# Attention stages of an encoder layer: TensorE order written by hand, softmax sums applied to the outputs

## The chip, the cores and the metric

The kernel runs on one core of one Trainium2 chip, in one launch. The metric is the device time of a run in microseconds (us). The kernel before has a median of 2528.19 us over three runs (2527.29 to 2535.42). Its profiled execution took 2528.55 us, of which the program's instructions span 2526.8 us; all rows below are of that execution.

## The reference

One post-norm encoder layer is applied to two sequences with the same weights: a prompt of 512 tokens and a sample of 1024, both 1024 wide. Per sequence:

```
u     = layernorm(x) * (1 + sc1) + sh1                  # modulation from silu(c) @ w_ada
proj  = u @ w_in  -> qa ka va (8 heads on 2 kv heads of 64) | qb kb vb (8 heads) | ga gb
oa    = softmax(rope(rms(qa)) . rope(rms(ka)) / 8) @ va          # over all tokens ("gqa")
ob    = softmax(qb . kb / 8 + bias) @ vb                          # over an 8 x 16 window ("na")
mixed = (sigmoid(ga) * (oa @ w_out_a) + sigmoid(gb) * (ob @ w_out_b)) @ w_out
x     = layernorm(alpha * x + (1 + g1) * mixed) * g + b
x     = layernorm(alpha * x + (1 + g2) * (relu(mod(x) @ w_ff1) ** 2 @ w_ff2)) * g + b
```

The softmax is `p / sum(p)`; whether the division comes before or after the product with v changes no value but rounding.

## The kernel before, in words

Work is in chunks of 512 tokens: one of the prompt, two of the sample. To keep fp32 precision each matrix product is three products of a high and a low half (`mm3`, L110): `hi*hi`, `hi*lo`, `lo*hi`, 512 columns each, accumulated in one PSUM bank. A weight unit is 128x1024 fp32; `wunit` (L81) loads it on SP's queue, ScalarE rounds it to `whi` (L93), VectorE subtracts for `wlo` (L94). `stream` (L97) keeps one unit ahead.

Every stage is a Python generator that yields its progress, and `weave` (L46) always advances the one that is furthest behind. That fixes the order in which instructions are recorded. The order on each engine is then set at build time by a scheduler that keeps a list of ready instructions by priority, so TensorE's order need not be the recorded one. At run time every engine works through its own list in order and waits on semaphores.

The stages, in order of time:

- Up to 171 us: modulation, and `proj` (L412) of the prompt.
- Stage 1, 171 to 285 us (L1008): `sample_u`, the layer norm and 64 transposes (L167) of the sample; `gates` (L492) of the prompt; `mod_rest`, 22 more modulation columns on VectorE.
- Stage 2, 285 to 640 us (L1023): attention of the prompt, woven with `proj` of the two sample chunks. `gqa` (L503) runs to 470 us, `na` (L598) from 490 us.
- Stage 3, 640 to 1163 us (L1040): attention of the sample, woven with its `gates` and with `out_merge` (L726) of the prompt. `gqa` runs to 942 us, `na` from 968 us.
- After 1163 us: merge, mix and norm of the rest, and the feed-forward layer.

In `gqa` a block is one head and 512 queries. For each of its four query tiles, `softmax` (L528) makes the scores `S` (L535: 2 products of 512 columns per 512 keys), the row maximum `m` on VectorE (L538), the exponential on ScalarE with its row sum `z` (L541), the reciprocal (L542), and multiplies the probabilities `P` by it, in turn on VectorE (L544) and ScalarE (L546). `values` (L549), for each 128 keys of the block before, turns four 128x128 tiles of `P` on TensorE (L553, tile `T`), splits the result into `ph` and `pl` (L556, L557), and multiplies with `V` into `A` (L566, L567).

In `na` an item is one head, 8 rows and 16 columns of the token grid (32 items in the prompt, 64 in the sample). GpSimd adds table and mask to the bias `wm` (L647), three items ahead. `softmax` (L651) makes 2 score products of 256 (prompt) or 384 columns (L658), the sum with the bias and its maximum on VectorE (L661, L662), the exponential (L665), the reciprocal (L666) and the scaling of `P` (L667, VectorE). `values` (L670) turns 2 or 3 tiles (L674), ScalarE copies them to `pt` (L676), and `weigh` (L679) multiplies with `V` (L681, fp32, two records per product in the trace). After four items VectorE copies the result to `o` (L686).

Fill work, that is `proj` and `gates`, has four PSUM banks in stage 2 and three in stage 3 (L1015, L1027). All writes of `g`, `oa` and `ob` are issued by SP.

Of the kernel before, what the change touches and what calls it, by code (L numbers as in the profile page):

```python
# [1 line left out]

# [8 lines left out]
F32 = mybir.dt.float32  # L11
# [21 lines left out]
GL = 0.06  # L33
AHEAD = 1
GQ = (0.55, 0.55)
AT = (1.1, 0.94)
# [3 lines left out]
class Kern:  # L40
# [4 lines left out]
    @staticmethod  # L45
    def weave(*gens):  # L46

        live = [[0.0, i, g] for i, g in enumerate(gens)]
        while live:
            e = min(live)  # L50
            try:
                e[0] = next(e[2]) or 0.0
            except StopIteration:
                live.remove(e)

# [59 lines left out]

    def dps(self):
        return self.psD.tile([P, CH], F32, tag="D", name="D")
# [44 lines left out]
    def mod_tile(self, pool, xns, s, sh0, sc0, kt, vector=False):  # L162

        nc = self.nc
        ps = self.dps()
        for t in range(TT):
            nc.tensor.transpose(ps[:, t * P:(t + 1) * P], xns[t][:, kt * P:(kt + 1) * P], self.ident)  # L167
        u = pool.tile([P, CH], F32, tag="uf", name="uf", bufs=3)
# [5 lines left out]
        return u  # L174
# [118 lines left out]
    def u_tile(self, seq, xns, pool, upool, U, kt):  # L293
        nc = self.nc
        u = self.mod_tile(pool, xns, seq, 0, 8, kt, seq == 0)
# [4 lines left out]
        U.append((uh, ul))  # L300


    def tokmajor(self, U, ws, kper, n, ps):
# [3 lines left out]
        for j in range(nu):  # L307
# [3 lines left out]
            for t in range(TT):  # L311
                for i in range(kper):
                    k = j * kper + i
                    uh, ul = U[k]
                    self.mm3(ps[t][:, :n], (uh[:, t * P:(t + 1) * P], ul[:, t * P:(t + 1) * P]),
                             (hv[:, i, :], lv[:, i, :]), k == 0, k == KT - 1)
            yield
# [9 lines left out]
    def stack(self, pool, src, dsts, scale=None, perm=False):  # L327

        nc = self.nc
        for j in range(2):  # L330
            t = pool.tile([P, CH], F32R, tag="stk", name="stk", bufs=3)
# [74 lines left out]
    def pair_stack(self, pool, q2s, hp, dsts):  # L406
        ps = self.dps()
        for t in range(TT):
            self.nc.tensor.transpose(ps[:, t * P:(t + 1) * P], q2s[t][:, hp * P:(hp + 1) * P], self.ident)
        self.stack(pool, ps, dsts)  # L410

    def proj(self, ch, U, pool):  # L412
# [4 lines left out]
        ws = self.stream([a["wq"][i] for i in range(4)] + [a["wkv"][i] for i in range(2)]  # L417
                         + [a["wst"][i] for i in range(8)] + [a["wvb"][i] for i in range(4)])
# [3 lines left out]
        for _ in self.tokmajor(U, ws, 2, 512, ps):  # L422
            done += 1
            yield done / 18.0
# [9 lines left out]
        for _ in self.tokmajor(U, ws, 4, 256, ps):  # L434
            done += 1
            yield done / 18.0
# [25 lines left out]
        todo = {2: [(q_rope, 0)], 3: [(q_rope, 1), (k_rope, 0)], 4: [(q_rope, 2), (k_rope, 1)],  # L462
                5: [(q_rope, 3), (k_rope, 2)], 6: [(k_rope, 3)],
                7: [(q_stack, 0)], 8: [(q_stack, 1)], 9: [(q_stack, 2)], 10: [(q_stack, 3)], 11: [(k_stack, 0)]}
        for i in range(8):
            ps = self.wstat(next(ws), [U])[0]
# [4 lines left out]
            if i == 2:  # L471
# [5 lines left out]
        ps = []  # L477
        for j, _ in enumerate(self.tokmajor(U, ws, 2, 512, ps)):
            for f, x in todo.get(8 + j, ()):
                f(x)  # L480
            done += 1
            yield done / 18.0
        for t in range(TT):
            v = pool.tile([P, CH], F32, tag="vb", name="vb", bufs=2)
            nc.scalar.activation(v, ps[t], AF.Copy)
            r = t0 // GW + 2 * t
            for hp in range(4):
                for i in range(2):
                    c0 = (r % 4 + i) * GW
                    nc.sync.dma_start(s["vb"][hp][c0:c0 + GW, r // 4], v[i * GW:(i + 1) * GW, hp * P:(hp + 1) * P])  # L490

    def gates(self, chs, Us, pool, func):  # L492
        nc, a = self.nc, self.a
        for i, w in enumerate(self.stream(a["wst"][8 + i] for i in range(16))):
            ps = self.wstat(w, Us)
            for (seq, t0), p in zip(chs, ps):
                g = pool.tile([P, CH], F32, tag="gst", name="gst", bufs=2)
                nc.scalar.activation(g, p, func)
                nc.sync.dma_start(self.scr[seq]["g"][i][:, t0:t0 + CH], g)
# [3 lines left out]
    def gqa(self, seq, pool, psp):  # L503
# [6 lines left out]

        def load(kv, h):
            if kv is not None and kv not in KV:
                K = []
                for r in range(2):
                    k = pool.tile([P, T], F32R, tag=f"K{r}", name="K", bufs=1)
# [10 lines left out]
            return KV[kv][0] if kv is not None else None, Qs[h]  # L526

        def softmax(blk, qt):  # L528
            kv, h, qc = blk
            K, Q = load(kv, h)  # L530
            S = psp.tile([P, T], F32, tag="S", name="S", bufs=2 if nh == 1 else 1)
            q = Q[:, qc * CH + qt * P:qc * CH + (qt + 1) * P]
            for k in range(nh):
                for r in range(2):
                    nc.tensor.matmul(S[:, k * CH:(k + 1) * CH], q, K[r][:, k * CH:(k + 1) * CH],  # L535
                                     start=r == 0, stop=r == 1)
            m = pool.tile([P, 1], F32, tag="m", name="m", bufs=4)
            nc.vector.tensor_reduce(m, S[:, :T], axis=AX.X, op=ALU.max, negate=True)  # L538
            p = pool.tile([P, T], F32, tag="P", name="P", bufs=8 if nh > 1 else 7)
            z = pool.tile([P, 1], F32, tag="z", name="z", bufs=4)  # L540
            nc.scalar.activation(p, S[:, :T], AF.Exp, bias=m, scale=1.0, accum_out=z)  # L541
            nc.vector.reciprocal(z, z)  # L542
            if qt % 2:
# [645 lines left out]
```

## Time and profile before

| | |
|---|---|
| profiled execution / its span | 2528.55 us / 2526.8 us |
| TensorE busy (mean granted clock) | 2388.2 us, 95% (0.975) |
| VectorE / ScalarE / GpSimd busy | 1472.3 / 971.3 / 330.1 us (58 / 38 / 13%) |
| stages 1, 2, 3 | 114, 355, 523 us |

Busy time of TensorE is the union of its matmul records. Records of successive matmuls overlap, so a busy TensorE can still run below its best rate, and the cost of one product is read from the distance between starts, not from its record's length. The granted clock is a share of full speed: 1.00 is the level of 2.4 GHz, and a half is that of 1.2 GHz.

### The profile page before, as it was taken

How to read it: one execution, taken by the hardware profiler on the slowest of the kernel's cores; microseconds unless marked ns; L12 is line 12 of the kernel's file. 1: busy time of each engine (PE TensorE's matmuls, PEld its weight loads, DVE VectorE, ACT ScalarE, POOL GpSimd, SP SyncE). 2: the span in 40 equal slices, each digit the busy share in tenths (PEclk: the TensorE clock that was granted, in tenths of full speed). 3: DMA queues.
4: the chain of work that ended last, by engine and by line, in shares of the span. 5: the costliest groups of instructions: out<-in, count | busy, mean ns of one | idle time of the engine just before them, and what ended most of it. 6: DMA issues, size and time to landing. Idle time of an engine off the chain costs nothing.

```text
span 2526.8 us, 29800 instructions
## 1 busy us (share of the span) xinstructions
PE 2388.2 (95%) x10992; PEld 1898.6 (75%) x10992; DVE 1472.3 (58%) x2511; ACT 971.3 (38%) x1589; POOL 330.1 (13%) x278
## 2 busy tenths in 40 slices
PE   5987899979999999989998999999999999999997
PEld 4876777756777777767776788887788888888876
DVE  7987677565477763575867754445733333333466
ACT  4434456434577763554334223222412211221222
POOL 4210021230000003331202000003100000000133
PEclk9998899989999999999999999999999999999999
DMA  6757744565512117585656525334511210211231
GB/s 248 245 185 238 213 119 145 141 187 174 157 55 66 58 50 184 148 235 189 202 188 206 191 69 159 99 90 126 176 40 45 61 48 26 67 50 34 68 116 59
DMA packets 134851, 325.86 MB, mean 129 GB/s; under 512 B 21392, under 2 KB 34224, under 8 KB 134704
## 3 DMA queue, kind: packets, MB, share of 16 engines
q1 hardware_dynamic: 134128, 322.86, 41.8%
q0 software_dynamic: 288, 1.05, 0.3%
q8 instruction: 87, 1.43, 0.2%
q14 instruction: 60, 0.49, 0.1%
q10 hardware_dynamic: 288, 0.03, 0.0%
HBM read 261.99 MB, written 62.93 MB: 129 GB/s over the span
## 4 chain that ended last, share of the span: by engine, by line
PE 68%; DVE 12%; DMA 8%; issue 4%; ACT 3%; POOL 2%; SPq 1%; POOLq 0%; ACTq 0%; DVEq 0%
PE D L112 18%; PE D L114 18%; PE D L113 18%; PE S L535 3%; PE T L553 3%; DVE wlo L94 2%; PE A L681 2%; PE A L566 2%; PE A L567 1%; DMA wraw<-in_wada 1%; PE T L674 1%; DVE junk L248 1%; DMA wraw<-in_wst 1%; ACT whi L93 1%; PE S L658 1%
## 5 line engine op out<-in xcount | busy, mean ns | idle before, releaser
L93 ACT ACTIVATE whi<-wraw 128x1024 fp32r<-128x1024 f32 x266 | 279.4, 1057 | 828.2 <-PE D L114 396.9
L114 PE MATMUL D<-uh,wlo 128*128 128x512 f32 x1344 | 537.2, 400 | 20.5 <-DVE wlo L94 20.5
L112 PE MATMUL D<-uh,whi 128*128 128x512 f32 x1344 | 538.3, 400 | 14.1 <-ACT whi L93 12.5
L113 PE MATMUL D<-ul,whi 128*128 128x512 f32 x1344 | 533.9, 397 | 0.0
L94 DVE TENSOR_TENSOR wlo<-wraw,whi 128x1024 fp32r<-128x1024 f32 x266 | 334.8, 1261 | 336.5 <-ACT whi L93 325.8
L114 PEld LDWEIGHTS D<-uh,wlo 128*128 128x128 f32 x1344 | 256.5, 191 | 78.9 <-DVE wlo L94 23.0
L112 PE MATMUL D<-whi,hh 128*128 128x512 f32 x768 | 304.8, 398 | 6.3 <-ACT hh L864 6.3
L112 PEld LDWEIGHTS D<-uh,whi 128*128 128x128 f32 x1344 | 257.3, 191 | 70.1 <-ACT whi L93 13.8
L114 PE MATMUL D<-whi,hl 128*128 128x512 f32 x768 | 303.7, 397 | 0.8 <-DVE hl L865 0.6
L113 PE MATMUL D<-wlo,hh 128*128 128x512 f32 x768 | 303.4, 397 | 0.0
L113 PEld LDWEIGHTS D<-ul,whi 128*128 128x128 f32 x1344 | 257.0, 191 | 54.7 <-issue 0.5
L886 DVE TENSOR_TENSOR y<-y,D 128x512 f32<-128x512 f32 x168 | 115.1, 685 | 214.8 <-PE D L114 214.2
L112 PEld LDWEIGHTS D<-whi,hh 128*128 128x128 f32 x768 | 145.4, 189 | 43.8 <-ACT hh L864 10.2
L114 PEld LDWEIGHTS D<-whi,hl 128*128 128x128 f32 x768 | 145.3, 190 | 37.3 <-DVE hl L865 3.7
L113 PEld LDWEIGHTS D<-wlo,hh 128*128 128x128 f32 x768 | 145.5, 189 | 33.6
L847 POOL TENSOR_TENSOR y<-y,g 128x1024 f32<-128x1024 f32 x12 | 28.8, 2402 | 867.4 <-DVE y L886 867.4
L538 DVE TENSOR_REDUCE m<-S 128x1 f32<-128x1024 f32 (+1 forms) x96 | 99.7, 1041 | 51.7 <-PE S L535 51.2
L557 DVE TENSOR_TENSOR pl<-T,ph 128x512 fp32r<-128x512 f32 x160 | 107.4, 684 | 16.4 <-ACT ph L556 15.0
L556 ACT ACTIVATE ph<-T 128x512 fp32r<-128x512 f32 x160 | 93.4, 597 | 55.5 <-PE T L553 53.1
L112 PE MATMUL D<-whi,uh 128*128 128x512 f32 (+1 forms) x288 | 105.5, 371 | 2.8 <-ACT whi L93 2.2
L647 POOL TENSOR_TENSOR wm<-Wb,mask 128x384 f32<-128x384 f32 (+1 forms) x96 | 78.4, 830 | 198.4 <-DVE m L661 118.8
L113 PE MATMUL D<-wlo,uh 128*128 128x512 f32 (+1 forms) x288 | 103.6, 360 | 0.0
(159 smaller groups left out, 3700.1 us busy)
## 6 DMA issues: line engine op xcount, KB each, us to landing
wraw<-in_w SPq DMA_DIRECT2D x132, 512.0 KB, 3.7
wraw<-in_wst SPq DMA_DIRECT2D x56, 512.0 KB, 5.4
wraw<-in_wada SPq DMA_DIRECT2D x32, 512.0 KB, 4.3
g<-gst SPq DMA_DIRECT2D x48, 256.0 KB, 2.3
og<-g SPq DMA_DIRECT2D x48, 256.0 KB, 3.2
wraw<-in_wab SPq DMA_DIRECT2D x24, 512.0 KB, 5.2
wraw<-in_wo SPq DMA_DIRECT2D x24, 512.0 KB, 5.1
raw<-in_wada_k SPq DMA_DIRECT2D x16, 512.0 KB, 8.2
```

The costliest lines, as they stand in the source:

```text
L93: nc.scalar.activation(hi, raw, AF.Copy)
L94: (engine or nc.vector).tensor_tensor(lo, raw, hi, op=ALU.subtract)
L112: mm(out, l[0], r[0], start=start, stop=False)
L113: mm(out, l[0], r[1], start=False, stop=False)
L114: mm(out, l[1], r[0], start=False, stop=stop)
L535: nc.tensor.matmul(S[:, k * CH:(k + 1) * CH], q, K[r][:, k * CH:(k + 1) * CH], start=r == 0, stop=r == 1)
L538: nc.vector.tensor_reduce(m, S[:, :T], axis=AX.X, op=ALU.max, negate=True)
L553: nc.tensor.transpose(tp[:, qt * P:(qt + 1) * P], Ps[qt][:, k * P:(k + 1) * P], self.ident)
L556: nc.scalar.activation(ph, tp, AF.Copy)
L557: nc.vector.tensor_tensor(pl, tp, ph, op=ALU.subtract)
L647: nc.gpsimd.tensor_tensor(wm.rearrange("p (r c) -> p r c", c=32), wv, mask[:, rt * 4 + b, :].rearrange("p (r c) -> p r c", c=32), op=ALU.add)
L886: nc.vector.tensor_tensor(y[:, hs], y[:, hs], ps, op=ALU.add)
```

## The change

Three things change together.

1. In stages 1 to 3 TensorE's order is no longer the scheduler's: `in_order` records the weave under a manual schedule for TensorE, so that it runs exactly in the recorded order. The generators now yield after each product (`mm3s`), and `share` turns a count of yields into progress. In `gqa` and `na` score products, transposes and value products are small closures that are called in turn, one transpose, then one wide product; the transposes of `proj` (`pair_stack`) wait in a list, and one is taken after each product of `mm3s`. Softmax, splits and finishes are recorded at high priority for the other engines. The turns of `na` stand two items behind the scores (one before), its value products three.
2. `P` is no longer scaled. Four row sums are kept as a 128x4 tile `Z`, inverted once, written to DRAM by ScalarE's queue (`za`, `zb`: 512 values of 4 bytes in a transposed order), and read back on GpSimd's queue, spread over 64 partitions (`zr`). The output `o` (64x512) is multiplied by it: on GpSimd in `gqa` and in `na` of the prompt, on VectorE straight from PSUM in `na` of the sample.
3. Around it: `proj` does the values of `na` (wvb) first instead of last; the writes of `g`, `oa` and `ob` go from SP's queue to GpSimd's; `gqa` gets a second `S` tile in the sample (third bank in the prompt) and the fill one PSUM bank instead of three in stage 3, and a second one during `na`; the progress constants are new.

The core of the diff:

```diff
-GL = 0.06
-GQ = (0.55, 0.55)
-AT = (1.1, 0.94)
+GQ = (0.55, 0.58)
+AT = (1.02, 0.96)
+LEAD = (0.06, 0.12)
+NLEAD = (0.14, 0.16)
+GAP = 8
+HP = 1000
...
+    def in_order(self, *gens):
+
+        with self.tc.manual_schedule(engines={mybir.EngineType.PE}):
+            self.weave(*gens)
...
+    def mm3s(self, out, l, r, start, stop):
+
+        mm = self.nc.tensor.matmul
+        for i, (x, y) in enumerate(((l[0], r[0]), (l[0], r[1]), (l[1], r[0]))):
+            mm(out, x, y, start=start and i == 0, stop=stop and i == 2)
+            if self.small:
+                self.small.pop(0)()
+            yield
...
-                nc.sync.dma_start(self.scr[seq]["g"][i][:, t0:t0 + CH], g)
+                nc.gpsimd.dma_start(self.scr[seq]["g"][i][:, t0:t0 + CH], g)
+                for _ in range(GAP if len(self.psD) == 1 else 0):
+                    yield
...
-            nc.vector.reciprocal(z, z)
-            if qt % 2:
-                nc.vector.tensor_scalar(p, p, z, None, op0=ALU.mult)
-            else:
-                nc.scalar.activation(p, p, AF.Copy, scale=z)
-            return p
+                nc.scalar.activation(p, S[:, :T], AF.Exp, bias=m, scale=1.0, accum_out=z[:, qt:qt + 1])
+                if qt == TT - 1:
+                    nc.vector.reciprocal(z, z)
+                Ps[blk].append(p)
...
+            o = pool.tile([64, CH], F32, tag="o", name="o", bufs=1)
+            nc.vector.tensor_tensor(o, a[0:64], t, op=ALU.add)
+            nc.gpsimd.tensor_tensor(o, o, zr.pop(blk), op=ALU.mult)
+            nc.gpsimd.dma_start(s["oa"][h * 64:(h + 1) * 64, qc * CH:(qc + 1) * CH], o)
...
+                    for x in (small, big):
+                        if n < len(x):
+                            x[n]()
+                    yield lead + (1.0 - lead) * (i + (j + (n + 1.0) / TT) / kq) / (steps + 1)
+                with self.tc.high_priority(HP):
+                    if split:
+                        split()
...
+            if nrt > 1:
+                nc.vector.tensor_tensor(ov, v(acc[0:64]), zv, op=ALU.mult)
...
+        def norms(h, rt):
+            zr[h, rt] = pool.tile([64, CH], F32, tag="zr", name="zr", bufs=1)
+            nc.gpsimd.dma_start(zr[h, rt], s["zb"][h][rt * CH:(rt + 1) * CH].partition_broadcast(64))
...
+            if i >= 1 and i - 1 < n and items[i - 1][2] == 3:
+                h, rt = items[i - 1][:2]
+                nc.scalar.dma_start(s["zb"][h][rt * CH:(rt + 1) * CH].rearrange("(b p) -> p b", p=P), Z.pop((h, rt)))
+
+            big, softmax = scores(*items[i]) if i < n else ([], None)
+            small, copy = turns(ps.pop(0)) if 2 <= i < n + 2 else ([], None)
+            for j in range(max(len(big), len(small))):
+                for x in (big, small):
+                    if j < len(x):
+                        x[j]()
+                with self.tc.high_priority(HP):
+                    if softmax and j == 1:
+                        ps.append(softmax())
+                    if copy and j == ng - 1:
+                        pts.append(copy())
...
-        self.weave(attention(1), fill())
+        self.in_order(attention(1), fill())
```

TensorE in `na` of the prompt, before: `S` are scores, `T` turned probabilities, `A` value products, `D` the fill's bank.

```order
L114 MATMUL D<-uh,wlo 128x512
L112 MATMUL D<-uh,whi 128x512
L113 MATMUL D<-ul,whi 128x512
L114 MATMUL D<-uh,wlo 128x512
L658 MATMUL S<-K,Q 128x256 x2
L674 MATMUL T<-ident,P 128x128 x2
L681 MATMUL A<-pt,V 64x128 x2
L658 MATMUL S<-K,Q 128x256 x2
L681 MATMUL A<-pt,V 64x128 x2
L658 MATMUL S<-K,Q 128x256 x4
L112 MATMUL D<-uh,whi 128x512
L113 MATMUL D<-ul,whi 128x512
```

The same place after the change; the fill is at this point the keys and values of `gqa`, 256 columns wide.

```order
L791 MATMUL S<-K,Q 128x256
L815 MATMUL T<-ident,P 128x128
L142 MATMUL D<-whi,ul 128x256
L142 MATMUL D<-whi,uh 128x256
L142 MATMUL D<-wlo,uh 128x256
L142 MATMUL D<-whi,ul 128x256
L827 MATMUL A<-pt,V 64x128 x2
L142 MATMUL D<-whi,uh 128x256
L142 MATMUL D<-wlo,uh 128x256
L142 MATMUL D<-whi,ul 128x256
L791 MATMUL S<-K,Q 128x256
L815 MATMUL T<-ident,P 128x128
```

Before, items stand close together between long runs of fill; after, each item has its own share of fill, ten or eleven products.

GpSimd in `na` of the sample, before: `wm` is the bias, `og` belongs to `out_merge`, `mask` is the table's load.

```order
L647 TENSOR_TENSOR wm<-Wb,mask 128x256 x12
L607 DMA mask<-in_mask 128x3072
L647 TENSOR_TENSOR wm<-Wb,mask 128x384 x60
L756 TENSOR_TENSOR og<-og 128x512 x4
L647 TENSOR_TENSOR wm<-Wb,mask 128x384 x4
L756 TENSOR_TENSOR og<-og 128x512 x5
```

And after, for some eight items.

```order
L846 DMA zr<-zb_1_206 64x512
L777 TENSOR_TENSOR wm<-Wb,mask 128x384
L564 DMA g_1_191<-gst 128x512
L777 TENSOR_TENSOR wm<-Wb,mask 128x384
L841 DMA ob_210<-o 64x512
L777 TENSOR_TENSOR wm<-Wb,mask 128x384 x2
L846 DMA zr<-zb_1_206 64x512
L777 TENSOR_TENSOR wm<-Wb,mask 128x384 x2
L841 DMA ob_210<-o 64x512
L564 DMA g_1_191<-gst 128x512
L777 TENSOR_TENSOR wm<-Wb,mask 128x384 x2
```

The additions of the bias now share GpSimd's list with three kinds of DMA, each of which waits there for its data.

## Rows read from the trace of the kernel before

**Rows 1.** The page, part 1: busy us, share of the span, instructions.

```profile
PE 2388.2 (95%) x10992; PEld 1898.6 (75%) x10992; DVE 1472.3 (58%) x2511; ACT 971.3 (38%) x1589; POOL 330.1 (13%) x278
```

**Rows 2.** Busy time by stretch: window, length, engines, clock, DMA share, GB/s.

```profile
171.00:285.00 114.00, 98.03 (x437) 79.79 (x436) 83.61 (x133) 46.77 (x67) 1.02 (x1) 0.91 0.70 213
285.00:490.00 205.00, 194.15 (x977) 157.35 (x976) 131.28 (x235) 114.88 (x216) 44.33 (x43) 0.98 0.48 142
490.00:640.00 150.00, 127.50 (x576) 93.64 (x575) 82.23 (x238) 56.91 (x138) 32.82 (x44) 0.89 0.60 172
640.00:950.00 310.00, 309.18 (x1552) 240.43 (x1551) 215.02 (x316) 214.05 (x338) 0.64 (x1) 1.00 0.27 78
950.00:1163.00 213.00, 202.83 (x1084) 152.65 (x1083) 118.76 (x376) 95.93 (x227) 71.09 (x71) 0.98 0.67 180
...
2000.00:2200.00 200.00, 200.00 (x866) 162.63 (x865) 70.46 (x91) 41.90 (x58) 0.00 (x0) 1.00 0.17 48
```

**Rows 3.** Timeline of TensorE near 708 us: start, length, instruction; transposes in fours.

```profile
707.49 0.60 PE L553 MATMUL T<-ident,P 128*128 128x128 f32 x4
707.85 0.48 PE L566 MATMUL A<-ph,V 128*128 128x512 f32 x1
708.17 0.39 PE L567 MATMUL A<-pl,V 128*128 128x512 f32 x1
708.40 0.60 PE L553 MATMUL T<-ident,P 128*128 128x128 f32 x4
```

**Rows 4.** Timeline of TensorE near 749 us: one transpose between wide products.

```profile
748.98 0.39 PE L566 MATMUL A<-ph,V 128*128 128x512 f32 x1
749.21 0.27 PE L553 MATMUL T<-ident,P 128*128 128x128 f32 x1
749.24 0.48 PE L567 MATMUL A<-pl,V 128*128 128x512 f32 x1
749.55 0.71 PE L553 MATMUL T<-ident,P 128*128 128x128 f32 x5
```

**Rows 5.** Timeline of TensorE near 508 us: value products of the neighbourhood attention.

```profile
507.87 0.38 PE L674 MATMUL T<-ident,P 128*128 128x128 f32 x2
508.18 0.65 PE L681 MATMUL A<-pt,V 128*64 128x128 f32 x4
508.76 0.50 PE L113 MATMUL D<-ul,whi 128*128 128x512 f32 x1
509.10 0.40 PE L114 MATMUL D<-uh,wlo 128*128 128x512 f32 x1
```

**Rows 6.** TensorE's waits, 171 to 285 us: us in total, times, longest.

```profile
PE D L112 <- ACT whi L93: 11.4, 1, 11.4
```

**Rows 7.** TensorE's waits, 490 to 640 us.

```profile
PE S L658 <- DVE m L661: 5.8, 4, 4.3
PE T L674 <- DVE m L662: 3.4, 3, 1.2
```

**Rows 8.** Groups by line: count, busy us, mean ns, idle before.

```profile
L544 DVE TENSOR_SCALAR P<-P,z 128x1024 f32<-128x1024 f32 (+1 forms) x48 | 32.4, 674 | 1.4
L667 DVE TENSOR_SCALAR P<-P,z 128x384 f32<-128x384 f32 (+1 forms) x96 | 44.1, 460 | 2.2
L666 DVE RECIPROCAL z<-z 128x1 f32<-128x1 f32 x96 | 15.0, 157 | 15.1 <-ACT P L665 14.5
L546 ACT ACTIVATE P<-P,z 128x1024 f32<-128x1024 f32 (+1 forms) x48 | 48.3, 1006 | 6.0 <-DVE z L542 5.9
L647 POOL TENSOR_TENSOR wm<-Wb,mask 128x384 f32<-128x384 f32 (+1 forms) x96 | 78.4, 830 | 198.4 <-DVE m L661 118.8 <-DMA Wb<-in_rpb 55.9 <-DVE P L667 8.7
L382 POOL TENSOR_TENSOR q<-q,rt 128x512 f32<-128x512 f32 (+1 forms) x24 | 26.9, 1129 | 16.7 <-DVE q L381 16.3 <-DVE z L542 0.4
```

**Rows 9.** DMA issues: name, engine, count, KB each, median us to landing.

```profile
K<-kb SPq DMA_DIRECT2D x32, 256.0 KB, 6.2
vb<-vb SPq DMA_DIRECT2D x96, 32.0 KB, 1.9
```

More of the change, by code (lines that the diff above doesn't have):

```diff
@@ L476, in proj @@
             yield done / 18.0
[L477 to L490, printed above, removed]
+        self.drain()
     def gates(self, chs, Us, pool, func):
@@ L525, in load, with scores @@
                 Qs[h] = Q
-            return KV[kv][0] if kv is not None else None, Qs[h]
-        def softmax(blk, qt):
+        def scores(blk, qt):
             kv, h, qc = blk
-            K, Q = load(kv, h)
-            S = psp.tile([P, T], F32, tag="S", name="S", bufs=2 if nh == 1 else 1)
+            K, Q = KV[kv][0], Qs[h]
+            got = []
             q = Q[:, qc * CH + qt * P:qc * CH + (qt + 1) * P]
[L533 to L541, printed above, removed]
-            nc.vector.reciprocal(z, z)
-            if qt % 2:
-                nc.vector.tensor_scalar(p, p, z, None, op0=ALU.mult)
-            else:
-                nc.scalar.activation(p, p, AF.Copy, scale=z)
-            return p
@@ new lines, in scores, with turns, turn, split @@
+            return [partial(product, k, r) for k in range(nh) for r in range(2)], softmax
+        def turns(blk, k):
+            got = []
+            def turn(qt):
+                if not got:
+                    got.append(psp.tile([P, CH], F32, tag="ST" if nh == 1 else "T", name="T", bufs=3 if nh == 1 else 2))
+                nc.tensor.transpose(got[0][:, qt * P:(qt + 1) * P], Ps[blk][qt][:, k * P:(k + 1) * P], self.ident)
+            def split():
+                tp = got[0]
+                ph = pool.tile([P, CH], F32R, tag="ph", name="ph", bufs=2 + DEPTH + (nh > 1))
+                pl = pool.tile([P, CH], F32R, tag="pl", name="pl", bufs=2 + DEPTH + (nh > 1))
+                nc.scalar.activation(ph, tp, AF.Copy)
+                nc.vector.tensor_tensor(pl, tp, ph, op=ALU.subtract)
+                pend.append((blk, k, ph, pl))
+            return [partial(turn, qt) for qt in range(TT)], split
@@ L598, in na @@
+        while pend:
+            big, end = products()
+            for x in big:
+                x()
+                yield 1.0
+            if end:
+                finish(end)
     def na(self, seq, pool, psp):
@@ L649, in bias, with scores @@
             biases[h, rt, b] = wm
-        def softmax(h, rt, b):
+        def scores(h, rt, b):
             Q, K = load(h)
@@ new lines, in scores, with turns, turn, copy @@
+            return [partial(product, r) for r in range(2)], softmax
+        def turns(p):
+            got = []
+            def turn(g):
+                if not got:
+                    got.append(psp.tile([P, NK], F32, tag="T" if nrt > 1 else "ST", name="T", bufs=2 if nrt > 1 else 3))
+                nc.tensor.transpose(got[0][:, g * P:(g + 1) * P], p[:, g * P:(g + 1) * P], self.ident)
+            def copy():
+                pt = pool.tile([P, NK], F32, tag="pt", name="pt", bufs=3)
+                nc.scalar.activation(pt, got[0], AF.Copy)
+                return pt
+            return [partial(turn, g) for g in range(ng)], copy
@@ L730, in out_merge @@
         s = self.scr[seq]
+        ws = self.primed(self.stream(a["wab"][n] for n in range(KT)))
         O = []
```

367 lines of the change are left out of this document (231 added, 136 removed).

## The prediction

> **What bounds the kernel now.** I read the page first: TensorE is busy 95% of the span and nothing else comes near it [rows 1]. A faster VectorE or ScalarE can therefore save only what makes TensorE wait. The question is how much of TensorE's busy time is idle in disguise, and where. For that I read busy time by stretch, and then the timeline for the price of one product.
>
> The feed-forward stretch gives the price of a wide product: 866 in 200 us, 0.231 us each at full clock [rows 2]. The reader is to see next that a transpose of 128 columns costs much more than a quarter of it. Four transposes and two wide products take 708.40 - 707.49 = 0.91 us [rows 3], so a transpose costs (0.91 - 0.462) / 4 = 0.112 us. A single one between wide products: 749.55 - 748.98 = 0.57 us for two wide ones and it, 0.108 us [rows 4]. The value products of `na` are dearer: 1.23 us from 507.87 to 509.10 hold two transposes, one wide product and four such records [rows 5]; less 0.231 and 0.224 that is 0.775 us, or four at 0.112 and 0.33 us for entering and leaving the narrow shape. By columns (an estimate from 0.231) a score product of 256 costs 0.116 us and one of 384 costs 0.173 us.
>
> So an item of `na` is 2 x 0.116 + 2 x 0.112 + 0.775 = 1.23 us in the prompt, and 2 x 0.173 + 3 x 0.112 + (6 x 0.112 + 0.33) = 1.68 us in the sample. With the counts of [rows 2], split by kind as the program issues them, each stretch has a content and an excess:
>
> - 171 to 285: 377 wide, 60 transposes: 87.1 + 6.7 = 93.8 us; excess 20.2.
> - 285 to 490: 633 wide, 192 of 256 columns, 152 transposes: 146.2 + 22.3 + 17.0 = 185.5 us; excess 19.5.
> - 490 to 640: 300 wide, 20 transposes, 32 items: 69.3 + 2.2 + 39.4 = 110.9 us; excess 39.1.
> - 640 to 950: 1040 wide, 512 transposes: 240.2 + 57.3 = 297.5 us; excess 12.5.
> - 950 to 1163: 380 wide, 64 items: 87.8 + 107.6 = 195.4 us; excess 17.6.
>
> The sum is 108.9 us, and no order of the same products can give back more than that at these prices. A part of it is the clock: (1 - granted) x length is 10.3, 4.1, 16.5, 0 and 4.3 us, 35.2 us together [rows 2]. The rest is waiting. In 490 to 640 the longest wait is 4.3 us, for VectorE's `sb` of the next item (5.8 us in four waits), and turns wait 3.4 us [rows 7]: items run close together and each waits for its own softmax, then come long runs of fill. The stretch with the most transposes, 640 to 950, has clock 1.00: wide products between them are enough.
>
> **The change part by part.** TensorE executes the same products before and after, so only the excess can move.
>
> *Transposes one by one.* By [rows 3, 4] a single transpose costs 0.108 us where one of four costs 0.112: nothing gained, and I take zero. The row also says why: the wide product behind the transpose starts 0.03 us after it and then holds TensorE for 0.31 us instead of 0.231. The Trainium skill, page "TensorE: Matmul & The Clock Gate", section "Part 2: What happens when you issue a matmul", says that TensorE pulls weight loads ahead, so that the next tile's weights load while this one's product runs. Applied to a transpose between wide products this would hide its load and leave only its columns, which is the second rival below; the trace shows the load behind the short product not hidden.
>
> *490 to 640.* The hand order gives each item 11 fill products. An item then takes at most 1.23 + 11 x 0.231 = 3.8 us, and a turn comes two items after its scores, 7.6 us; the longest wait was 4.3 us [rows 7]. So those waits go, and with a steady mix the clock should behave as in 640 to 950. I keep 11 us for the entry into `na` (its mask, keys and bias load then) and leave 28 us of gain; bounds 10 and 36.
>
> *950 to 1163.* Before, the fill ran out while items remained. Now 408 wide products lie among the 64 items, 5 at most of them and one run of 97. Of 17.6 us I take 12; bounds -5 and 16, since the single fill bank and the late start of the merge can add waits.
>
> *285 to 490.* A third score bank and finer mixing; no row tells which wait ends last, so I take half, 9 us; bounds 0 and 15. What `proj` moves costs nothing while its last 24 wide products (5.5 us) and the 49 that lead the sample's `gqa` (11.3 us) cover write and reading back of the last heads, 12.4 us at the slowest landing [rows 9].
>
> *171 to 285.* One wait of 11.4 us for a weight unit is more than half of the excess [rows 6]; the DMA engines are 70% busy [rows 2]. The writes of `g` leave SP's queue, so a write that waits for its result no longer holds the loads behind it. They go to GpSimd's, idle here (1.02 us of 114). I take 6 us; bounds -5 and 15.
>
> *640 to 950.* Already dense. 2 us; bounds -8 and 8: with one fill bank the 8 blank steps between two accumulations must cover its release.
>
> *Sums and outputs.* VectorE loses 32.4 + 44.1 us of scaling and 144 reciprocals at 0.157 us, 22.6 us; ScalarE loses 48.3 us [rows 8]. This is 99 us of VectorE, but it lies beside TensorE, which stood at 309.18 of 310 us while VectorE had 215 [rows 2]: worth nothing by itself, it only makes the waits above easier to lose. GpSimd gains 32 multiplications of about 1.13 us (L382 has twice the partitions and the same length) [rows 8] and 144 DMA issues, and in 640 to 950 it has nothing else to do [rows 2]; if that cover is gone, the outputs come later, but they are read only after the stage. The two new trips through DRAM are bounded by the quickest and the slowest landing, 1.9 and 6.2 us each [rows 9]; with few bytes they are nearer to the 32 KB row, and I take 1.9. The late case is the last rival.
>
> Sum: 6 + 9 + 28 + 2 + 12 = 57 us. From the profiled execution, 2528.55 - 57 = 2471.6 us; the median lies 0.36 us below that execution, so 2471 us.
>
> **The rivals.**
>
> *Only the worst stretch pays.* If hand order only trades one wait for another elsewhere (TensorE in a fixed order stalls whole where a weight half or a bank is late, fill included), what is left is 490 to 640 with its 28 us: 2500 us. For it: the other excesses are small and partly prices I have only estimated. Against it: the clock and the run-out of fill are visible in two more stretches.
>
> *A transpose costs only its columns.* If a load hid on both sides, a transpose would cost 0.231 / 4 = 0.058 us, 0.054 less, and the 1000 transposes of the stages would give another 54 us: 2417 us. [rows 4] speaks against it, but that row is one spot in an order that seldom has single transposes.
>
> *It doesn't do what it says.* Waits are set by VectorE, ScalarE and DMA, and the new order meets them in other places: 2520 to 2536 us. Against it stands that these engines get lighter.
>
> *GpSimd's list becomes the bound in `na` of the sample.* Every four items it must add four biases, 4 x 0.83 = 3.3 us [rows 8], and stand at two DMAs: `zr` waits until `zb` has landed, `ob` until `zr` has landed and VectorE has used it. Behind them stand the biases of the next items, for which VectorE waits, and behind VectorE the turns. TensorE's pace is 1.68 + 5 x 0.231 = 2.84 us an item, 11.4 us for four. At 1.9 us a landing GpSimd needs 7.1 us: free. At 6.2 us it needs 15.7 us, 4.3 us over, 16 times: 69 us, and the time is 2540 us. It costs from (11.4 - 3.3) / 2 = 4.05 us a landing, and eats the whole gain from 5.8 us. Against it: GpSimd reaches `zr` after ScalarE issued `zb`, so it doesn't wait for all of the landing. The Trainium skill, page "DMA: Bandwidth & Descriptors", section "Anatomy of one DMA — SWDGE (gpsimd) path", gives a fixed cost of about 2.0 us a DMA, by which this rival would stay free; its section "Specifications" adds that transfers below 512 bytes are read, modified and written, which speaks for it, and no run here shows writes of 4 bytes.
>
> **How the numbers follow.** The forecast has 0.60; its five terms hardly miss to the same side, and their distances to the bounds, added as squares, give 15 us below and 30 us above: 2456 to 2501 us. Then only the worst stretch, 0.17; cheap transposes, 0.06; no change, 0.07; GpSimd's list, 0.10. A measurement of this kernel can tell 0.3%, 7.6 us, from no change. The first three are faster, 0.83; the fourth is the same, 0.07; the last is slower, 0.10. The range of 2428 to 2524 us leaves out the last case, the cheap transposes and most of no change.
>
> **What would show it.** Right: in the stretch of the prompt's `na` the granted clock above 0.97 and no wait for `sb` of some us; that stretch near 120 us; the sample's `gqa` no shorter in TensorE time per product; the scaling lines gone while TensorE's share rises to 97%. The single transposes, read as in [rows 4], still at 0.11 us. Wrong: a wide product after a transpose at 0.23 us; long waits of VectorE for `wm` or `zr`, and of TensorE for VectorE behind them; waits for `whi` or `wlo` in the woven stages, which would say that the priority of the softmax pushed the weights back; or a clock still at half level in the prompt's `na`.

## The result, and the profile after

The changed kernel takes 2760.2 us (median of 4 runs, 2759.0 to 2764.4) where the kernel before takes 2527.7 in the same comparison: 1.092 times as long, interval 1.089 to 1.095. The forecast was 2471, its range ended at 2524.

Page, part 1, of the profile after (answers [rows 1]):

```profile
PE 2431.5 (88%) x10992; PEld 1911.0 (69%) x10992; DVE 1401.8 (51%) x2223; ACT 930.7 (34%) x1541; POOL 447.7 (16%) x454
```

TensorE executes the same 10992 product records. Its share falls from 95 to 88% of a longer span, and no other engine has become the busiest: the time has gone into waiting. Windows by stage (columns as in [rows 2]): to the prompt's `gqa`, prompt `gqa`, prompt `na` up to the sample's start, sample `gqa`, sample `na`:

```profile
171.00:301.00 130.00, 122.67 (x538) 96.60 (x538) 100.57 (x151) 60.38 (x87) 8.92 (x16) 0.94 0.80 252
301.00:476.00 175.00, 145.07 (x687) 113.90 (x686) 98.31 (x157) 79.98 (x160) 50.57 (x57) 0.91 0.59 115
476.00:742.00 266.00, 193.77 (x889) 147.60 (x888) 103.93 (x224) 87.06 (x187) 69.00 (x81) 0.84 0.62 156
742.00:1014.00 272.00, 253.94 (x1335) 193.32 (x1333) 175.50 (x227) 166.91 (x285) 44.07 (x60) 0.99 0.26 56
1014.00:1371.00 357.00, 266.30 (x1218) 191.74 (x1218) 91.35 (x260) 101.25 (x235) 91.22 (x119) 0.84 0.54 116
```

The sample's `gqa` makes its first scores at 730 us instead of 653, and its `na` makes its last value product at 1368 instead of 1154. The time went into the two `na` stretches: TensorE is busy 194 of 266 us and 266 of 357 us there, at a granted clock of 0.84. Whom it waits for, the waits from 1050 to 1370 us show (us in total, times, longest):

```profile
POOL zr L846 <- DMA zb<-z: 158.7, 15, 18.6
DVE o L837 <- DMA zr<-zb: 148.5, 14, 18.0
ACT P L802 <- DVE m L797: 127.3, 16, 16.2
...
PE S L791 <- DVE m L796: 70.7, 14, 12.3
```

Read from the bottom up this is a chain: TensorE waits for VectorE's `sb`, VectorE for `zr`, GpSimd for `zb`. The timeline of one turn (start, length, instruction, idle before) shows that the chain is closed:

```profile
1113.72 0.37 ACTq L866 DMA_DIRECT2D zb<-z  x1
...
1124.90 0.53 POOL L846 DMA_DIRECT2D zr<-zb  x1 [9.23 <-DMA zb<-z]
...
1127.90 0.68 DVE L837 TENSOR_TENSOR o<-A,zr 64x512 f32<-64x512 f32 x1 [7.39 <-DMA zr<-zb]
1128.51 0.54 DVE L796 CUSTOM_DVE_ANT_0 sb<-S,wm 128x384 f32<-128x384 f32 x1
...
1129.28 0.61 ACT L802 ACTIVATE P<-sb,m 128x384 f32<-128x384 f32 x1 [5.80 <-DVE m L797]
...
1130.02 0.18 DVE L804 RECIPROCAL z<-z 128x4 f32<-128x4 f32 x1 [0.77 <-ACT P L802]
...
1130.23 0.37 ACTq L866 DMA_DIRECT2D zb<-z  x1
```

`zb` needs 11.2 us to land, `zr` 3.0. Only then comes `o`, and in VectorE's list `o` stands ahead of the `sb` of the next group's last item, whose row sum the next `zb` needs. This turn is 1130.23 - 1113.72 = 16.5 us for four items; by the prediction's estimate TensorE needs 11.4. It is one of the shorter ones: the fourteen turns from 1044.27 to 1311.63 us take 15.1 to 27.8 us, 19.1 on average.

In the prompt's `na` another queue shows. SP's list, and TensorE's longest wait there:

```profile
513.16 27.38 SPq L495 DMA_DIRECT2D vb<-vb  x32
540.58 0.58 SPq L753 DMA_DIRECT2D Q<-qb  x1
541.21 2.38 SPq L130 DMA_DIRECT2D K<-kb  x4
```

```profile
545.06 0.55 PE L791 MATMUL S<-K,Q 128*128 128x256 f32 x1 [16.77 <-DMA K<-kb]
```

The keys of the second head stand behind 32 writes of `vb`, which take SP 0.86 us each to issue.

One term of the forecast can be read at once, the single transpose, answering [rows 4] (timeline, sample `gqa`):

```profile
850.34 0.27 PE L631 MATMUL T<-ident,P 128*128 128x128 f32 x1
850.37 0.48 PE L607 MATMUL S<-K,Q 128*128 128x512 f32 x1
850.68 0.39 PE L142 MATMUL D<-ul,whi 128*128 128x512 f32 x1
850.91 0.27 PE L631 MATMUL T<-ident,P 128*128 128x128 f32 x1
```

One transpose and two wide products: 0.57 us, so 0.108 for the transpose, as before.

### The profile page after: what moved, and what is told of

Same layout as the page of the kernel before. It is cut to its first block, busy times and chain, and to the rows that moved or that the text cites. A ratio compares the mean times of both kernels' runs of the same rounds, so it can differ in the third digit from the quotient of the medians.

```text
span 2758.4 us, 29802 instructions
## 1 busy us (share of the span) xinstructions
PE 2431.5 (88%) x10992; PEld 1911.0 (69%) x10992; DVE 1401.8 (51%) x2223; ACT 930.7 (34%) x1541; POOL 447.7 (16%) x454
## 4 chain that ended last, share of the span: by engine, by line
PE 50%; DMA 16%; DVE 8%; issue 4%; ACT 3%; POOL 2%; SPq 1%; POOLq 0%; DVEq 0%; ACTq 0%
PE D L134 12%; PE D L136 12%; PE D L135 12%; DMA zb<-z 7%; PE D L142 6%; DMA zr<-zb 2%; PE A L651 2%; PE S L607 2%; PE T L631 2%; DVE wlo L116 2%; DMA K<-kb 1%; DMA wraw<-in_wst 1%; DMA Wb<-in_rpb 1%; ACT whi L115 1%; DVE og L926 1%
## 5 line engine op out<-in xcount | busy, mean ns | idle before, releaser
L116 DVE TENSOR_TENSOR wlo<-wraw,whi 128x1024 fp32r<-128x1024 f32 x266 | 341.3, 1285 | 372.0 <-ACT whi L115 371.5
L136 PE MATMUL D<-uh,wlo 128*128 128x512 f32 x768 | 301.6, 393 | 6.5 <-DVE wlo L116 6.5
L134 PE MATMUL D<-uh,whi 128*128 128x512 f32 x768 | 301.5, 393 | 0.2 <-ACT whi L115 0.2
L135 PE MATMUL D<-ul,whi 128*128 128x512 f32 x768 | 301.2, 392 | 0.0
L142 PE MATMUL D<-uh,whi 128*128 128x512 f32 x576 | 253.9, 441 | 17.9 <-ACT gst L563 9.0
L142 PE MATMUL D<-uh,wlo 128*128 128x512 f32 x576 | 252.3, 438 | 11.4 <-DVE wlo L116 11.3
L142 PE MATMUL D<-ul,whi 128*128 128x512 f32 x576 | 250.1, 434 | 0.0
L631 PE MATMUL T<-ident,P 128*128 128x128 f32 x640 | 173.9, 276 | 22.1 <-DVE pl L638 21.9
L136 PEld LDWEIGHTS D<-uh,wlo 128*128 128x128 f32 x768 | 144.6, 188 | 39.8 <-DVE wlo L116 7.8
L134 PEld LDWEIGHTS D<-uh,whi 128*128 128x128 f32 x768 | 144.7, 188 | 32.6 <-ACT whi L115 0.6
L135 PEld LDWEIGHTS D<-ul,whi 128*128 128x128 f32 x768 | 144.6, 188 | 31.8
L791 PE MATMUL S<-K,Q 128*128 128x384 f32 (+1 forms) x192 | 70.5, 368 | 105.3 <-DVE m L796 70.7
L607 PE MATMUL S<-K,Q 128*128 128x512 f32 x320 | 144.5, 480 | 15.4 <-ACT P L618 12.4
```

The costliest lines, as they stand in the source:

```text
L116: (engine or nc.vector).tensor_tensor(lo, raw, hi, op=ALU.subtract)
L134: mm(out, l[0], r[0], start=start, stop=False)
L135: mm(out, l[0], r[1], start=False, stop=False)
L136: mm(out, l[1], r[0], start=False, stop=stop)
L142: mm(out, x, y, start=start and i == 0, stop=stop and i == 2)
L607: nc.tensor.matmul(got[0][:, k * CH:(k + 1) * CH], q, K[r][:, k * CH:(k + 1) * CH], start=r == 0, stop=r == 1)
```

## The experiments

Times are medians. "Over before" is the ratio to the kernel before, timed in the same comparison, less one, times 2528 us; such figures are what I compare.

| run | edit | us | ratio (interval) | over before |
|---|---|---|---|---|
| after | | 2760 | 1.092 (1.089 to 1.095) | 233 |
| e1 | no sums | 2575 | 1.017 (1.016 to 1.019) | 43 |
| e2 | zr from elsewhere | 2662 | 1.052 (1.049 to 1.054) | 130 |
| e3 | z in runs of 16 B | 2595 | 1.025 (1.023 to 1.027) | 64 |
| e4 | wvb last | 2742 | 1.083 (1.081 to 1.086) | 211 |
| e5 | e1, wvb last | 2591 | 1.026 (1.023 to 1.029) | 64 |
| e6 | e1, z written, not read | 2664 | 1.054 (1.051 to 1.056) | 135 |
| e7 | before, sums alone | 2730 | 1.080 (1.077 to 1.083) | 203 |
| e8 | e1, scheduler's order | 2546 | 1.007 (1.005 to 1.010) | 18 |
| e9 | e7 in runs of 16 B | 2566 | 1.015 (1.013 to 1.018) | 39 |
| e10 | e1, hand order in stage 3 alone | 2567 | 1.017 (1.015 to 1.019) | 42 |
| e11 | before, division left out | 2524 | 0.999 (0.998 to 1.000) | -3 |
| e12 | e3, scheduler's order | 2555 | 1.012 (1.010 to 1.014) | 30 |
| e13 | e6, 128 pieces of 16 B | 2584 | 1.023 (1.020 to 1.026) | 58 |
| e14 | 4 pieces of 512 B | 2579 | 1.020 (1.018 to 1.023) | 51 |
| e15 | e8, wvb last | 2542 | 1.006 (1.003 to 1.008) | 14 |
| e16 | 512 pieces of 16 B | 2613 | 1.034 (1.030 to 1.038) | 85 |
| e17 | 128 pieces of 4 B | 2677 | 1.059 (1.055 to 1.063) | 149 |
| e17b | e6, 128 pieces of 4 B | 2641 | 1.046 (1.042 to 1.049) | 116 |

**Which half costs.** e1 scales `P` as before and drops `za`, `zb` and `zr`:

```diff
-                nc.scalar.activation(p, sb, AF.Exp, bias=m, scale=1.0, accum_out=z[:, b:b + 1])
...
+                nc.scalar.activation(p, sb, AF.Exp, bias=m, scale=1.0, accum_out=z)
+                nc.vector.reciprocal(z, z)
+                nc.vector.tensor_scalar(p, p, z, None, op0=ALU.mult)
```

> Hand order kept, the division of the outputs undone: P is scaled as in the kernel before, no za, zb, zr. Theory A (a closed loop: write of zb, its landing of some 11 us, read of zr of 3 us, o on VectorE, and behind o in VectorE's list the sb of the last item of the next four, whose row sum the next zb waits for; 16.4 us a turn where TensorE needs 11.4): the sample's na falls from 327 us to 185 to 210, the prompt's na loses the waits for zb (58.7 us on GpSimd, not all on the path), and the time is 2560 to 2610 us. Theory B (the hand order itself stalls TensorE, whoever it waits for): the sample's na stays over 270 us and the time over 2690.

Theory A holds: 2575 us, and the sample's `na` is back to 208 us (979 to 1187) from 327 (1044 to 1371). 190 of the 233 us go with the sums, 43 do not. e7 is the other half, the sums alone in the kernel before:

> The kernel before, with its scheduler's order, and only the sums moved to the outputs, by the same writes of 4 bytes and the same reads. Theory C + A (pieces hold up the transfers and the landing holds na, in any order of TensorE): slower than before, 2600 to 2720 us, the sample's na over 260 us. Theory E (the trip hurts only a TensorE that may not take other work meanwhile): 2520 to 2560 us.

203 us, and 2730 is 10 us above even theory C + A's range: the trip costs this in the scheduler's order too, and theory E falls.

**The wait or the write.** e2 leaves the writes and takes away the wait; its outputs are multiplied by a row of an input, so the division itself is left out:

```diff
-            nc.gpsimd.dma_start(zr[h, rt], s["zb"][h][rt * CH:(rt + 1) * CH].partition_broadcast(64))
+            nc.gpsimd.dma_start(zr[h, rt], a["lnmg"][0:CH].partition_broadcast(64))
```

> As the changed kernel, za and zb still written, but zr is read from a row of an input that is always there (the outputs are multiplied by that row instead of the inverse sums). Only the wait for the landing of zb and za is gone. Theory A: GpSimd's waits for zb are gone, VectorE's wait for zr falls from 157 us to under 30, the sample's na takes 185 to 215 us, the time is 2560 to 2620. Theory C (not the wait but the 25,000 writes of 4 bytes hold up the queues and the other DMAs): the time stays over 2700. Theory B: over 2690 too.

2662 lies between both forecasts: 103 of the 233 us go, 130 stay. So e6 takes e1 and adds the two writes, which nothing reads:

> As e1, but za and zb are written as in the changed kernel (512 pieces of 4 bytes from ScalarE's queue) and nobody reads them. Theory C (the pieces hold up the other transfers: 32 writes of vb took SP 34.9 us where e1 needed 20.5): 2630 to 2670 us, most of the 87 us between e1 and e2, and the sample's gqa again starts near 734 us instead of 674. If those 87 us come from reading zr and multiplying on GpSimd and VectorE: 2573 to 2595 us.

2664: 92 us over e1 for 48 writes of 2 KB whose result nothing reads. 57 of them are there at the sample's first scores (721 us, 664 in e1), and 26 more come in its `na` (234 us instead of 208). SP's first 32 `vb` writes of the sample, without (e1) and with them (e6):

```profile
310.83 20.50 SPq L495 DMA_DIRECT2D vb<-vb  x32
```

```profile
313.37 32.87 SPq L495 DMA_DIRECT2D vb<-vb  x32
```

SP takes 12 us longer to issue them, and whatever stands behind them comes later too. Nor is it SP's queue alone: on GpSimd's queue a write of `ob` lands after 8.0 us in e6 and after 2.6 in e1 (medians). The row of the queue that causes it (e6: packets, MB, share of 16 engines) doesn't betray it:

```profile
q10 hardware_dynamic: 25632, 0.13, 0.6%
```

**Pieces.** e3 writes each partition's four sums side by side, 128 runs of 16 bytes:

```diff
-...["zb"][h][rt * CH:(rt + 1) * CH].rearrange("(b p) -> p b", p=P), Z.pop((h, rt)))
+...["zb"][h][rt * CH:(rt + 1) * CH].rearrange("(p b) -> p b", p=P), Z.pop((h, rt)))
```

> As the changed kernel, but the sums are written as 128 runs of 16 bytes instead of 512 of 4 (the four sums of a partition side by side; the multiplication reads zr in that order). If the landing of zb goes with the number of pieces (theory A1), it falls from about 11 to 3 to 5 us, the loop takes 8 to 11 us a turn, under TensorE's 11.4, and the time is 2560 to 2630, near that of the kernel without the sums. If a write from ScalarE's queue lands late for another reason, whatever its pieces (theory A2), the landing stays at 9 us or more and the time over 2710.

> As e7 (the kernel before, its scheduler's order, only the sums moved to the outputs), but z written as 128 runs of 16 bytes. Theory C + A (pieces hold up transfers, a late landing holds na; both go with the number of pieces): from e7's 2730 down to 2530 to 2570 us. If the cost sits in the trip itself and not in its pieces: over 2680. If the lighter VectorE now shows: under 2515.

Theory A1 holds: 2595 us for e3, 2566 for e9, where e7 had 2730. A landing in e3:

```profile
1082.72 0.33 ACTq L867 DMA_DIRECT2D zb<-z  x1
...
1088.52 0.53 POOL L847 DMA_DIRECT2D zr<-zb  x1 [3.21 <-DMA zb<-z]
```

This one took 5.8 us; where GpSimd waited in the sample's `na` they lie between 1.9 and 9.8. Is it the number of pieces or their size? e13 writes e6's bytes in e3's shape; e14, e16 and e17 write from a constant tile (e14: 4 x 512 B, e16: 512 x 16 B, e17: 128 x 4 B).

> As e6 (hand order, sums undone, za and zb written and read by nobody), but each of the 48 writes goes in 128 runs of 16 bytes instead of 512 of 4. e1 without the writes takes 2575 us, e6 2664. Theory C1 (the cost goes with the number of pieces): a quarter of 89, 2590 to 2605 us. If it goes with the number of writes or of bytes: 2650 to 2670. If only pieces under some size cost: 2573 to 2583.

> As e13, but each write takes its 2 KB in 4 runs of 512 bytes from a tile that is always there, so their content isn't the sums; nobody reads them. Theory C1 (number of pieces): 2572 to 2582 us, like e1's 2575. If a write from ScalarE's queue costs by itself: 2590 or more.

> As e6, but each of the 48 unread writes has 512 pieces of 16 bytes, taken from a tile that is always there. e6 (512 of 4 bytes) takes 2664 us, e13 (128 of 16) 2584, e1 (none) 2575. Theory N (the number of pieces in a write decides): 2640 to 2690 us. Theory S (pieces under 16 bytes are what is slow): 2575 to 2600 us.

> As e16, but each write has 128 pieces of 4 bytes. Theory N: 2575 to 2592 us, like e13. Theory S: 2600 us or more.

e13 costs 15 us over e1. The intervals of the two leave some 9 us either way, so this run alone can't exclude that the cost goes with the number of pieces (a quarter of 92 is 23). The constant tile of e14, e16 and e17 was a mistake of design: nothing held those writes, and they were issued between 7 and 172 us, ahead of the attention stages (126 us, as the last expectation has it, is the end of `za` alone). So e14's 8 us over e1 say little. Among themselves e16 and e17 still speak, though e16's 2613 lies between its two ranges: four times fewer pieces, of 4 bytes, cost 106 us over e1 where those of 16 bytes cost 42. The last run, e17b, put pieces of 4 bytes back in their place (the write of `zb`; that of `za` is changed alike):

```diff
+                nc.scalar.dma_start(s["zb"][h][rt * CH:rt * CH + P].rearrange("(p e) -> p e", e=1), Z.pop((h, rt))[:, 3:4])
```

> Nothing in e16 and the run after it held their writes, and the traces show all of them between 7 and 126 us, not in the attention stages: 6144 pieces of 4 bytes cost 102 us there, 24576 of 16 bytes 38. This run writes the last of the four sums, 128 pieces of 4 bytes, where e6 and e13 write theirs. e13 (128 of 16 bytes, same places) took 2584 us, e6 (512 of 4) 2664. Theory S (a piece of 4 bytes is dear, one of 16 is not, so price times number): about 2575 + 89/4 = 2597, 2592 to 2610 us. Theory S2 (any write with 4-byte pieces costs the same, whatever the number): 2640 to 2670. Theory N (number alone): 2578 to 2590.

2641, 72 us over e1: theory S2. In the same places and number, 128 pieces cost 72 us at 4 bytes and 15 at 16; four times as many pieces of 4 bytes (e6) add only 20. The landing of the `za` writes themselves, and that of the keys on SP's queue, e13 first, then e17b:

```profile
DMA to landing us min/median/max: 1.4/1.7/2.4
K<-kb SPq DMA_DIRECT2D x32, 256.0 KB, 5.8
```

```profile
DMA to landing us min/median/max: 6.9/7.2/8.1
K<-kb SPq DMA_DIRECT2D x32, 256.0 KB, 17.6
```

So the transfers of the other queue are slower too, not only their issue. SP's list says the same, again e13 first:

```profile
314.12 20.51 SPq L495 DMA_DIRECT2D vb<-vb  x32
```

```profile
313.22 31.75 SPq L495 DMA_DIRECT2D vb<-vb  x32
```

Why 4 bytes are dear and 16 are not, no run shows: in e13 and e17b alike the pieces of one write lie side by side in DRAM, so the length of a piece isn't told apart from the number of pieces in the same stretch of memory.

**The hand order.** e8 takes e1 and drops the manual schedule (`in_order` only weaves); e10 drops it in stage 2 alone.

> As e1, but TensorE's order in stages 1 to 3 is left to the scheduler again; generators, lags, banks, queues and constants stay as changed. e1 lies 44 us over the kernel before. Theory B1 (the fixed order is what costs: TensorE stands at a late operand while other work is ready): 2525 to 2555 us. Theory B2 (the single fill bank, the order in proj and the places of the loads cost): 2565 to 2600 us.

> As e1 (2575), but only stage 3, the sample's attention, keeps the hand order; stage 2, the prompt's, is left to the scheduler (with e8, all three left: 2546). Reading the traces, the hand order loses where operands come late from SP's list: in the prompt's na (waits of 10 and 11 us) and, by waits for pl, 16 us in the sample's gqa. Theory B3 (both stages lose): 2555 to 2566 us. If only the prompt's stage loses: 2544 to 2553. If only the sample's: 2568 to 2580.

e8 is at 18 us over before: the fixed order costs 25 us. e10's 2567 lies between the ranges for both stages and for the sample's alone, and its ratio is e1's. Its sample makes its first scores at 654 us, like e8's (653; e1 664), but these 10 us are gone by the end. So in the total time the 25 us go with the stages that e10 leaves fixed, 1 and 3, and stage 1 isn't it, for the prompt's first scores come at 297 us in e1 and at 301 in e8. Windows of the sample's `gqa` in e1 and in e8, and the wait in e1 that goes with it:

```profile
674.00:950.00 276.00, 257.45 (x1347) 195.20 (x1346) 203.44 (x305) 198.99 (x319) 17.59 (x30) 0.99 0.16 49
```

```profile
665.00:920.00 255.00, 252.25 (x1343) 197.62 (x1343) 200.42 (x306) 196.63 (x320) 16.83 (x29) 1.00 0.17 52
```

```profile
PE T L632 <- DVE pl L639: 15.7, 14, 2.0
```

Nearly the same products take 21 us more. For 15.7 us of them TensorE stands, up to 2.0 us at a time, at a transpose whose bank VectorE has not yet released by `pl`; in its fixed order it can take nothing else meanwhile. e8 has 1.9 us of this wait in its window.

**The place of wvb.** e4, e5 and e15 put the values of `na` last in `proj` again.

> As the changed kernel, but proj does the values of na (wvb) last again, as before. In the changed kernel 32 writes of vb take 27.4 us of SP's queue from 513 to 541 us, and the keys of the prompt's second na head, issued behind them, make TensorE wait 16.8 us. Theory D (this wait is on the path): the prompt's na and the start of the sample's gqa come 15 to 35 us earlier, time 2720 to 2745. If the stage is held by the sums' loop anyway: 2750 to 2765. If the writes at the end of proj delay the sample's na instead: over 2765.

> As e1 (hand order, sums undone), and proj does wvb last again. In e1 two waits of TensorE in the prompt's na, 10.1 us for the keys of the second head and 11.0 us for a whi whose load stood behind them, both follow 32 writes of vb that hold SP's list for 22 us. Theory D (these two are part of what the hand order costs): 2550 to 2566 us, the two waits gone. If other waits take their place: 2568 to 2582 us, like e1's 2574.8.

> As e8 (sums undone, the scheduler's order; 2546 us, 20 over the kernel before), and proj does wvb last again. In e8 the first 100 us hold 300 matmul records where the kernel before has 433, and the writes of vb again fall into the start of the prompt's na. Theory B4 (the place of wvb is what is left): 2522 to 2535 us. If it sits in the single fill bank and the constants: 2540 to 2560.

With the sums (e4) it saves 22 us, as theory D has it. Without them D falls: e5 is 21 us slower than e1, above both of its ranges. TensorE's waits in e5, 285 to 740 us, show why:

```profile
PE S L607 <- DMA Q<-qa: 16.9, 1, 16.9
...
PE D L142 <- DVE grow L314: 14.5, 1, 14.5
...
PE S L786 <- DMA K<-kb: 3.2, 2, 2.6
```

Most of the wait for the keys went, and the sample's first queries became late in its place (16.9 us at 679 us). In the free order (e15) the place is worth some 4 us, within the intervals.

The place also matters where nothing above looked, before 171 us. With wvb first, 32 writes of the prompt's `vb` stand in SP's list ahead of the next weights; SP's list and TensorE in e1:

```profile
71.38 20.59 SPq L495 DMA_DIRECT2D vb<-vb  x32
92.07 1.00 SPq L110 DMA_DIRECT2D wraw<-in_wq  x2
```

```profile
97.12 1.22 PE L142 MATMUL D<-whi,uh 128*128 128x512 f32 x2 [16.88 <-ACT whi L115]
```

By 171 us e1 has executed 626 product records where the kernel before has 703; e8 waits 16.8 us at the same place. e15 doesn't have this wait, but loses the gain again in stages 1 and 2: TensorE waits 10.7 us for a weight half at 196 us, behind 32 writes of `vb` (168 to 190 us), and 11.3 us for the sample's queries at 658. The 14 to 18 us left in the free order I leave open: the single fill bank, the constants and the queues were not tried one by one.

**What the best case is.** e11 multiplies the outputs, but takes the factor from a tile loaded once per part, so it leaves the division itself out; e12 takes both costs down in the changed kernel.

> The kernel before with P unscaled and no trip at all: the outputs are multiplied by a tile that is loaded once in each part, so the division by the sums is left out. It shows what the moved division could give at best. By the prediction (99 us of VectorE beside TensorE are worth nothing by themselves): 2515 to 2530 us, at most the waits behind VectorE gone. If the scaling of P was a hidden bound: under 2505. If multiplying outputs on GpSimd and VectorE costs by itself: over 2535.

> The changed kernel with its two costs taken down: z in runs of 16 bytes and TensorE's order left to the scheduler. If both costs add (e3 lies 20 us over e1, and e8 29 us under it): 2555 to 2575 us. If a free order also hides what is left of the landing: 2535 to 2552 us. If the relief of VectorE pays in a free order: under 2530.

e11 is no faster than before that can be told. VectorE is busy 1397.8 us in it (1472.3 in [rows 1]) and TensorE, as before, sets the time. e12 is still 30 us over: 18 from e8, 12 from the trip. No run beats the kernel before by more than its interval, and by e11 no cheaper trip would make the moved division pay there.

## Why the prediction was wrong

The 233 us, as differences of the ratios: 18 of banks, constants and places (e8), 25 of the fixed order (e1 over e8), 92 of the writes (e6 over e1), 97 of waiting for their landing and reading them back (after over e6).

- **The step that failed** is the price of the new trips: "with few bytes they are nearer to the 32 KB row, and I take 1.9." Bytes were the wrong measure. `zb` landed after 11.2 us in the turn above and 21.0 at worst (issued at 1044.27, `zr` released at 1065.28); my upper end of 6.2 us, the slower of [rows 9], was too low as well. I noted that no run shows writes of 4 bytes, and then bounded them by rows of pieces more than a hundred times as long.
- **What no step had**: that a write can slow transfers of another queue which don't wait for it. Those 92 us are in none of the rivals.
- The last rival had the place and the wait ("long waits of VectorE for `wm` or `zr`, and of TensorE for VectorE behind them"). Its formula with the landings of the turn above gives 3.3 + 11.2 + 3.0 = 17.5 us a group, near the 16.5 of that turn, but partly by luck: the turn is closed by VectorE's list and not by GpSimd's, which issues its biases while `zr` is under way. The sample's `na` takes 327 us where e6, with the same writes and no wait for them, takes 234; these 93 us are nearly all of the 97. With 6.2 us the rival was priced too low, and given one chance in ten.
- The Trainium skill ("DMA: Bandwidth & Descriptors", "Anatomy of one DMA — SWDGE (gpsimd) path") has a fixed cost of about 2.0 us a DMA for the path from GpSimd, which is `zr`'s; `zb` goes from ScalarE's queue, for which that section states nothing. The 3.0 us of `zr` are not far from it; `zb` took 1.4 to 9.1 us in pieces of 16 bytes (e13) and 7.5 to 14.2 in pieces of 4 (e17b). The rule of the same page of the Trainium skill ("Specifications") on transfers below 512 bytes spoke for the right side, but of the two sizes written in place here 4 bytes were dear and 16 cost little.

The forecast gains can be read from e1 and e8, which leave the sums alone. As in the prediction, a stretch's excess is its length less its products at the prediction's prices, so these figures are estimates (the products of four columns up to 171 us count at their records' length). Each run has its own bounds: before 171, 285, 474, 669, 942, 1156; e1 171, 297, 480, 674, 950, 1190; e8 171, 300, 484, 665, 920, 1119.

| stretch, us | gain forecast | excess before | e1 | e8 |
|---|---|---|---|---|
| up to 171 | none | 41 | 57 | 59 |
| to the prompt's `gqa` | 6 | 21 | 12 | 15 |
| the prompt's `gqa` | 9 | 20 | 22 | 17 |
| the prompt's `na`, to the sample's `gqa` | 28 | 41 | 55 | 46 |
| the sample's `gqa` | 2 | 11 | 26 | 6 |
| into the sample's `na`, and it | 12 | 18 | 17 | 6 |
| the rest | none | 65 | 75 | 85 |

- **490 to 640, 28 us of gain**: wrong. The waits for `sb` of [rows 7] did go (e1 has none there), but keys and a weight unit, late behind SP's list, cost 10.8 and 13.7 us instead, and the clock is 0.89 in e1 (480 to 674) where it was 0.91 (474 to 669), not above 0.97. e1 takes 194 us for that stretch and the kernel before 195, but with 749 product records against 797. This is my first rival's mechanism, "hand order only trades one wait for another"; it was priced as if it could only eat gains.
- **640 to 950, 2 us of gain**: wrong sign in the hand order. The bound of -8 allowed for waits for the fill bank; what came is the wait for `pl`, 15.7 us, and the excess rose by 15. In the free order of e8 it fell by 5.
- **950 to 1163, 12 us**: hardly any of it. In e1 the items themselves have an excess of 9 us (980 to 1190) instead of 18, but the 30 us ahead of them have 8 where before had none.
- **171 to 285, 6 us**: the excess fell by 9, but by luck and not by the mechanism named. The wait of 11.4 us for a weight unit [rows 6] went from here because wvb went to the front, not because the writes of `g` left SP's queue: with wvb last again e15 and e5 have 10.7 and 10.3 us of it here, their `g` on GpSimd's queue. The wait has moved to 97 us, where it takes 16.9, and e1 reaches the prompt's `gqa` at 297 us and not at 285.
- **285 to 490, 9 us**: no gain in the hand order; e1 takes 183 us instead of 189, but with 827 product records against 877.
- **Terms put at nothing without a reason**: the stretch before 171 us, where e1 loses 16 us by the place of wvb (with it last again, e15 has an excess of 43 there), and the one after the sample's `na`, where e1 loses 10 and e8 20. In the stages between, e8 has 21 us less excess than the kernel before, so a part of the forecast 57 us is there in the free order; it is lost ahead of them and behind them. Why the last part takes longer stays open.
- **Right**: a transpose costs 0.108 us in any order, so rival two falls; and VectorE's relief is worth nothing by itself (e11, 0.998 to 1.000).

## What to carry to other kernels

Price a transfer by the length of its contiguous pieces before its bytes, and ask what it does to the queues beside it: here writes that nothing reads cost as much (92 us) as the wait for them (97). Where a result travels through memory, follow the list of each engine that uses it until it comes back to the producer; if it does, the whole landing is in the loop. A hand-written order of the busiest engine stands at each late operand: here 15.7 us at transposes, where a scheduler's order of the same products stood 1.9. And look at the stretches that a change reaches without being meant for them.

## What the runs showed of the hardware that I had not expected

- Writes with pieces of 4 bytes from ScalarE's queue made SP's queue slower: 32 writes took 32.9 us to issue (e6) instead of 20.5 (e1), with 0.6% of the DMA engines' time in the page of the profile for the queue that did it. At 16 bytes a piece it was 20.5 again (e13).
- The transfers beside them landed later: the keys on SP's queue after 17.6 us (e17b, 4 bytes) instead of 5.8 (e13, 16 bytes), `ob` on GpSimd's after 8.0 (e6) instead of 2.6 (e1).
- Of 128 pieces each, a write of `za` landed after 7.2 us at 4 bytes a piece (e17b) and after 1.7 at 16 (e13).
- The cost grew little with the number of such pieces: 72 us for 48 writes of 128 (e17b), 92 us for 48 of 512 (e6).
